# Empty slots' rows left out of an expert gather, and low parts moved from VectorE to GpSimd, in a two-block layer stack on one core

## The chip, the core and the metric

The kernel runs on one core of a Trainium2 chip. The time is that of one execution on the device, in microseconds; a kernel's time is the median of several runs. Of the core's engines, PE (TensorE) multiplies, DVE (VectorE), ACT (ScalarE) and POOL (GpSimd) work elementwise, and SP issues most loads. Each engine runs its own stream of instructions in order and waits on semaphores for the others. DMAs from the queues of SP, ACT and POOL run beside them.

## The reference, cut to what matters

Two blocks of a model work on 512 tokens of 1024 features in float32. The first block is attention of two kinds, cross-attention into a memory, and a mixture of experts; the second begins with a gated delta stage (with a short convolution and a memory attention of its own), followed by a feed-forward network, windowed attention and another network. The change touches the mixture of experts and the beginning of the delta stage.

```python
# experts: 4 groups of 8; each token takes one group and two experts in it
expert_ids = (g_sel * EXPERTS_PER_GROUP + e_sel).reshape(-1)      # 512 tokens x 2
def block_fn(args):
    tok, wt, e = args
    xb = h_pad[tok]                                   # the rows of one expert's tokens
    hidden = jax.nn.silu(xb @ w_gate[e]) * (xb @ w_up[e])
    return (hidden @ w_down[e]) * wt[:, None].astype(hf.dtype)
out = jnp.zeros((n_tok + 1, d), hf.dtype).at[slot_token].add(y.reshape(n_slots, d))[:n_tok]
x = x + out
x = rms_norm(x, norm_final_g)          # end of the first block
h = rms_norm(x, ln_mix_2)              # start of the second; its products with w_gdn and the small w_gdn_ba
```

(The last two lines are written in short; in the reference each norm stands in its own function.) An empty slot has no token, and its weight is zero.

## The kernel before, in words

Features lie on the partitions: the state x is eight tiles of 128 x 512 (feature chunk by token). Products are made nearly in float32 out of three products of rounded numbers: `split` (lines 404 to 411) takes a tile into a rounded high part (`hi`, on ACT) and the difference (`lo`, on DVE or on the engine that its argument names), and `mm3` (397 to 402) multiplies high by high, low by high and high by low. Weights come as tiles of 128 x 1024 (512 KB) through a ring of buffers; `use` makes their parts, `blk` runs one output tile of 128 x 512 over the eight chunks. A scheduler of the framework places each engine's instructions by dependences and by its own estimate of times; `issue_after(i)` holds what is written inside it back behind instruction i on the same engine.

**The mixture of experts** (`moe`, from line 1393). The router's product, then the choice of experts on DVE. Each expert has 64 slots, 2048 in all; two pairs of experts share a call of `slots`: on DVE four comparisons `G` (128 x 256, an iota against the tokens' positions), on PE eight small products `pm` that bring each slot its token number and weight, on DVE the token numbers `idx`, and on POOL two indirect DMAs that read the slots' token rows (128 rows of 4 KB each) from a copy of x in DRAM. An empty slot reads row 0. `gather` transposes these rows (`pgt`) on PE. Beside the choice of experts stand keys and values of a memory for the second block, for two layers (`mem_kv2`, 833 to 838): PE computes them, and they fill the time in which PE would have nothing. Then a branch (line 1697) tests for an expert with more than 64 tokens. The loop over experts follows: eight passes, each with four experts, `gate_up` (`pgu`), `down` (`py`), and `scatter` (`psx`), which adds the results to x through one-hot matrices `S`; DVE adds each `psx` into x (line 1651). Of the experts' weights, `NPRE` tiles are loaded ahead of the routing.

**The start of the delta stage** (`gdn`, from line 840). `two_norms` (from line 456) computes the statistics of two norms in one go: ACT squares the eight chunks (`sqt`), PE sums them (`sum`, line 471, two columns wide), DVE and POOL make the factors `rt`, and PE and DVE spread them to a row `rbc`. Meanwhile `xh` and `xl` are the parts of x for the products. `few` (from line 535) is the small product with `w_gdn_ba` (16 matmuls of 128 x 512, line 544), whose copy `fewo` is transposed (line 549). Then come the blocks with `w_gdn`; a block's result is multiplied with `rbc` into `pad` (944). The first blocks are not held. The second block of the stage has its first half behind the last sum product and its second half behind the product that makes `rbc` (`gates`, lines 525 to 528). Both results of `few` are put in the two banks (`pmm`) that the blocks use as well. The exponential `ea` of ACT (line 912) needs another function table than the squares.

## Time and profile before

| what | value |
|---|---|
| median of three runs | 2013.53 us (2011.08 to 2014.74) |
| the profiled execution | 2020.15 us |
| its span | 2018.4 us |
| mean granted clock of TensorE | 0.974 |
| PE busy (weight loads) | 96% (73%) |
| DVE, ACT, POOL busy | 51%, 37%, 18% |
| the chain that ended last | PE 69%, DVE 4%, ACT 2%, DMA 2% |
| DMA | 253.89 MB, mean 126 GB/s |

The profiled execution takes 1.75 us more than its span, which begins with the first instruction and ends with the last. The clock of TensorE has two levels, and the mean of 0.974 says that it was at the lower one for a twentieth of the time. A busy PE does not mean a PE at its best; a stretch must be looked at with its clock.

### The profile page before, as it was taken

How to read it: one execution, taken by the hardware profiler on the slowest of the kernel's cores; microseconds unless marked ns; L12 is line 12 of the kernel's file. 1: busy time of each engine (PE TensorE's matmuls, PEld its weight loads, DVE VectorE, ACT ScalarE, POOL GpSimd, SP SyncE). 2: the span in 40 equal slices, each digit the busy share in tenths (PEclk: the TensorE clock that was granted, in tenths of full speed). 3: DMA queues.
4: the chain of work that ended last, by engine and by line, in shares of the span. 5: the costliest groups of instructions: out<-in, count | busy, mean ns of one | idle time of the engine just before them, and what ended most of it. 6: DMA issues, size and time to landing. Idle time of an engine off the chain costs nothing.

```text
span 2018.4 us, 25671 instructions
## 1 busy us (share of the span) xinstructions
PE 1932.1 (96%) x9678; PEld 1471.1 (73%) x9678; DVE 1030.9 (51%) x2091; ACT 746.6 (37%) x1494; POOL 361.6 (18%) x344
## 2 busy tenths in 40 slices
PE   8999999979999999999998999999999999999997
PEld 6768677754444467878877888888866688888886
DVE  7674655643332367788856433343436654334434
ACT  5554643621212233345544322232335642222331
POOL 3012241200000003444412110111111021101111
PEclk9988999979999979999999999999999999999999
DMA  5213115259999832111122322332321033233322
GB/s 194 63 53 120 42 54 203 82 189 387 409 408 409 337 107 85 53 43 53 43 74 80 97 89 89 115 94 80 108 73 33 30 100 101 75 104 112 94 78 71
DMA packets 78911, 253.89 MB, mean 126 GB/s; under 512 B 9208, under 2 KB 12352, under 8 KB 78784
## 3 DMA queue, kind: packets, MB, share of 16 engines
q1 hardware_dynamic: 73520, 240.34, 34.7%
q0 software_dynamic: 2448, 8.43, 1.1%
q10 hardware_dynamic: 2816, 3.44, 0.5%
q8 instruction: 78, 1.28, 0.3%
q14 instruction: 49, 0.40, 0.1%
HBM read 243.75 MB, written 8.39 MB: 125 GB/s over the span
## 4 chain that ended last, share of the span: by engine, by line
PE 69%; DVE 4%; ACT 2%; DMA 2%; issue 1%; POOL 1%; DVEq 0%; ACTq 0%
PE mmp L400 16%; PE mmp L401 16%; PE mmp L402 16%; PE pgu L1599 6%; PE py L1599 3%; PE psx L1648 3%; DMA raw<-in_w_swa_dram 1%; PE sc L1327 1%; PE po L749 1%; DVE lo L408 1%; PE pgt L1446 1%; PE tp L961 1%; PE po L1353 1%; ACT hi L407 1%; PE pt L1339 1%
## 5 line engine op out<-in xcount | busy, mean ns | idle before, releaser
L400 PE MATMUL mmp<-xh,hi 128*128 128x512 f32 (+1 forms) x1328 | 522.1, 393 | 1.3 <-ACT xh L407 0.7
L401 PE MATMUL mmp<-xl,hi 128*128 128x512 f32 (+1 forms) x1328 | 516.0, 389 | 1.0 <-DVE xl L411 1.0
L402 PE MATMUL mmp<-xh,lo 128*128 128x512 f32 (+1 forms) x1328 | 516.1, 389 | 0.0
L407 ACT ACTIVATE hi<-raw 128x1024 fp32r<-128x1024 f32 (+2 forms) x256 | 252.1, 987 | 645.8 <-PE mmp L401 556.9
L408 DVE TENSOR_TENSOR lo<-raw,hi 128x1024 fp32r<-128x1024 f32 (+1 forms) x242 | 279.0, 1154 | 150.2 <-ACT hi L407 147.6
L400 PEld LDWEIGHTS mmp<-xh,hi 128*128 128x128 f32 x1328 | 252.0, 190 | 57.6 <-issue 5.7
L401 PEld LDWEIGHTS mmp<-xl,hi 128*128 128x128 f32 x1328 | 252.2, 190 | 50.1 <-DVE xl L411 1.4
L402 PEld LDWEIGHTS mmp<-xh,lo 128*128 128x128 f32 x1328 | 251.7, 190 | 50.2 <-issue 0.7
L808 POOL TENSOR_TENSOR g<-g,rbc 128x512 f32<-128x512 f32 x44 | 75.2, 1708 | 508.8 <-ACT g L807 508.8
L400 PE MATMUL mmp<-ahi,hi 128*128 128x512 f32 (+1 forms) x374 | 141.9, 380 | 0.0
L401 PE MATMUL mmp<-alo,hi 128*128 128x512 f32 (+1 forms) x374 | 141.9, 380 | 0.0
L402 PE MATMUL mmp<-ahi,lo 128*128 128x512 f32 (+1 forms) x374 | 141.9, 379 | 0.0
L434 POOL TENSOR_TENSOR sqt<-sqt 128x512 f32<-128x512 f32 (+1 forms) x50 | 70.0, 1399 | 255.9 <-ACT sqt L430 239.7
L810 DVE TENSOR_TENSOR a<-mmp,g 128x512 f32<-128x512 f32 x44 | 30.4, 691 | 144.4 <-PE mmp L402 144.4
L806 DVE TENSOR_TENSOR g<-mmp,rbc 128x512 f32<-128x512 f32 x44 | 30.4, 691 | 112.8 <-PE mmp L402 112.7
L401 PEld LDWEIGHTS mmp<-alo,hi 128*128 128x128 f32 x374 | 70.4, 188 | 14.1
L400 PEld LDWEIGHTS mmp<-ahi,hi 128*128 128x128 f32 x374 | 70.4, 188 | 14.0
L402 PEld LDWEIGHTS mmp<-ahi,lo 128*128 128x128 f32 x374 | 70.4, 188 | 14.0
L1599 PE MATMUL pgu<-raw,xh 128*64 128x512 f32 x256 | 61.0, 613 | 4.0 <-PEq L1697 4.0
L1599 PE MATMUL py<-raw,act 128*64 128x512 f32 x256 | 58.9, 596 | 1.0 <-ACT act L1626 1.0
L1599 PE MATMUL pgu<-raw,xl 128*64 128x512 f32 x256 | 57.2, 595 | 0.0
L410 ACT ACTIVATE xh<-py,msl 128x512 fp32r<-128x512 f32 x32 | 22.0, 688 | 94.8 <-PE py L1599 94.8
(519 smaller groups left out, 2969.6 us busy)
## 6 DMA issues: line engine op xcount, KB each, us to landing
raw<-in_w_egu_dram SPq DMA_DIRECT2D x128, 512.0 KB, 10.2
raw<-in_w_gu_dram SPq DMA_DIRECT2D x88, 512.0 KB, 3.5
raw<-in_w_ed_dram SPq DMA_DIRECT2D x64, 512.0 KB, 10.2
raw<-in_w_out_dram SPq DMA_DIRECT2D x24, 512.0 KB, 3.5
raw<-in_w_gdn_dram SPq DMA_DIRECT2D x24, 512.0 KB, 3.6
raw<-in_w_dn_dram SPq DMA_DIRECT2D x32, 384.0 KB, 3.1
raw<-in_w_dn_dram SPq DMA_DIRECT2D x32, 320.0 KB, 2.8
raw<-in_w_qk_dram SPq DMA_DIRECT2D x12, 512.0 KB, 4.3
```

The source lines that it names most:

```text
L400: mm(ps, a[0], b[0], start=first, stop=False)
L401: mm(ps, a[0], b[1], start=False, stop=False)
L402: mm(ps, a[1], b[0], start=False, stop=last)
L407: nc.scalar.activation(hi, src, AF.Copy)
L408: (eng or nc.vector).tensor_tensor(lo, src, hi.bitcast(F32), OP.subtract)
L410: nc.scalar.activation(hi, src, AF.Copy, scale=scale)
L434: (nc.vector if i == len(chunks) - 1 else nc.gpsimd).tensor_tensor(acc, acc, s, OP.add)
L806: nc.vector.tensor_tensor(g, pg, bc, OP.mult)
L808: nc.gpsimd.tensor_tensor(g, g, bc, OP.mult)
L810: nc.vector.tensor_tensor(a, pu, g, OP.mult)
L1599: m = nc.tensor.matmul(ps[hb], a[:, hb], w[b][:, o:o + 512], start=first, stop=last)
L1648: m = nc.tensor.matmul(psx, ys[k][:, a, c * P:(c + 1) * P], ss[a], start=a == part[0] and k == 0, stop=a == part[-1] and k == 1)
```

## The change

It has six parts.

1. In `slots` an empty slot gets the index 1023 instead of 0, and the indirect DMA checks its indices against 511 and skips a row beyond it. The row tiles are now fixed ones, set to zero once on POOL: two before the first gather, four behind the branch.
2. `mem_kv2` runs the first layer's keys and values early, and holds the second layer's keys behind the count product, its values behind the first `pm` products. The second layer's four low parts are made on POOL.
3. `NPRE` is 14 instead of 12.
4. In the delta stage the low parts of `w_gdn_ba` and of the first two tiles of `w_gdn` are made on POOL.
5. `few` is written inside `two_norms`' pool of banks and has a bank of its own there; the blocks' first half has no gate, the second half stands behind the last sum product.
6. `ea` is held behind the last Square.

```diff
-NPRE=12
+NPRE=14
...
-            self.split(hi, lo, t, eng=self.lo_eng)
+            self.split(hi, lo, t, eng=self.nc.gpsimd if self.lo_first else self.lo_eng)
+            self.lo_first = max(0, self.lo_first - 1)
...
-                if self.nblk == 2:
+                if self.nblk == 2 and self.loose:
+                    if c * 2 >= kc:
+                        st.enter_context(self.tc.issue_after(self.gates[0]))
+                elif self.nblk == 2:
...
-    def few(self, w, hs, pool):
+    def few(self, w, hs, pool, bank=None):
...
-        self.split(st[:, :, 0:64], st[:, :, 64:128], raw)
-        ps = self.pmm.tile([P, T], F32, name="mmp", tag="mm")
+        self.split(st[:, :, 0:64], st[:, :, 64:128], raw, eng=self.nc.gpsimd if self.lo_first else None)
+        bank = bank or (lambda name: self.pmm.tile([P, T], F32, name=name, tag="mm"))
+        ps = bank("mmp")
...
-    def mem_kv2(self, m):
+    def mem_kv2(self, m, l, gates):
...
-        for l in range(2):
-            self.mem_keys(m, d[f"w_mem_k2{l}"], 256, self.kv2d[l])
-            self.mem_values(m, d[f"w_mem_v2{l}"], 256, self.kv2d[l])
+        for g, f, w in zip(gates, (self.mem_keys, self.mem_values), (f"w_mem_k2{l}", f"w_mem_v2{l}")):
+            with self.tc.issue_after(g) if g else ExitStack():
+                f(m, d[w], 256, self.kv2d[l])
...
                 hs, rt, rbc, r1bc = self.two_norms("norm_final_g", "ln_mix_20", q, gp)
+                self.lo_first = 2
+                pba = self.few(d["w_gdn_ba"], hs, gp, lambda name: q.tile([P, T], F32, name=name, tag="few"))
...
-                nc.scalar.activation(ea, rows[:, 6:12], AF.Exp)
+                with tc.issue_after(self.squared):
+                    nc.scalar.activation(ea, rows[:, 6:12], AF.Exp)
...
+                far = gq.tile([P, 2], F32, name="far", tag="far", bufs=3)
+                nc.vector.tensor_scalar(far, ms[:, :, 4], 0.0, 1024.0, op0=OP.is_equal, op1=OP.mult)
                 idx = gq.tile([P, 2], I32, name="idx", tag="idx", bufs=3)
-                nc.vector.tensor_scalar(idx, ms[:, :, 4], 1.0, 0.0, op0=OP.subtract, op1=OP.max)
-                rows = []
+                self.idx = nc.vector.scalar_tensor_tensor(idx, ms[:, :, 4], -1.0, far, op0=OP.add, op1=OP.add).ins
                 for a in range(2):
-                    r = room() if room else gr.tile([P, D], F32, name="rows", tag="rows")
-                    nc.gpsimd.indirect_dma_start(r, None, tokd, bass.IndirectOffsetOnAxis(idx[:, a:a + 1], 0))
-                    rows.append(r)
+                    nc.gpsimd.indirect_dma_start(rows[a], None, tokd, bass.IndirectOffsetOnAxis(idx[:, a:a + 1], 0),
+                                                 bounds_check=T - 1, oob_is_err=False)
...
+                    self.mem_kv2(m2, 0, (None, None))
...
+                first = [r1.tile([P, D], F32, name=f"rows{a}") for a in range(2)]
+                for t in first:
+                    nc.gpsimd.memset(t, 0.0)
...
-                sl = slots(0, lambda: r1.tile([P, D], F32, name="rows", tag="rows", bufs=2), ps)
+                sl = slots(0, first, ps)
                 if self.on("gdn"):
-                    self.mem_kv2(m2)
+                    self.lo_eng = nc.gpsimd
+                    self.mem_kv2(m2, 1, (counts, self.pm))
+                    self.lo_eng = None
...
-            gr = e(name="mr", bufs=4)
+            gr = e(name="mr", bufs=1)
+            room = [gr.tile([P, D], F32, name=f"row{a}") for a in range(4)]
+            for t in room:
+                nc.gpsimd.memset(t, 0.0)
```

How this moves the instructions shows at three places. The first is POOL's stream in the routing, before the change: `sqt` and `rt` belong to norms, `rows` are the gathered rows, and `flag` is the branch's test.

```order
L434 TENSOR_TENSOR sqt<-sqt 128x256
L419 TENSOR_TENSOR rt<-rp,mhalf 128x4
L434 TENSOR_TENSOR sqt<-sqt 128x256 x5
L419 TENSOR_TENSOR rt<-rp,mhalf 128x2
L1430 DMA rows<-tokd,idx 128x1024 x2
L1696 TENSOR_LOAD flag
```

The same place after it:

```order
L437 TENSOR_TENSOR sqt<-sqt 128x256
L422 TENSOR_TENSOR rt<-rp,mhalf 128x4
L437 TENSOR_TENSOR sqt<-sqt 128x256 x5
L422 TENSOR_TENSOR rt<-rp,mhalf 128x2
L411 TENSOR_TENSOR lo<-raw,hi 128x1024 x4
L1438 DMA rows_3966<-tokd,idx 128x1024
L1438 DMA rows_3967<-tokd,idx 128x1024
L1713 TENSOR_LOAD flag
```

Four low parts now stand ahead of the two row DMAs. The second place is DVE's stream in the routing, before: `As` and `posm` are the tokens' positions in their experts, `mk` the copied keys, `msl` the slots' data.

```order
L408 TENSOR_TENSOR lo<-raw,hi 128x1024
L1559 TENSOR_TENSOR meta<-wt,meta 128x16x2 x4
L408 TENSOR_TENSOR lo<-raw,hi 128x1024
L1544 TENSOR_SCALAR As<-As 128x128
L1545 TENSOR_TENSOR posm<-pl,As 128x128
L1547 TENSOR_REDUCE mx<-posm 128x1
L1414 TENSOR_TENSOR G<-cst_moe,posm 128x256 x4
L694 TENSOR_TENSOR mk<-mmp,rbc 128x256
L1414 TENSOR_TENSOR G<-cst_moe,posm 128x256 x4
L408 TENSOR_TENSOR lo<-raw,hi 128x1024
L1550 TENSOR_REDUCE mx<-pl 1x1
L694 TENSOR_TENSOR mk<-mmp,rbc 128x256
```

After:

```order
L1571 TENSOR_TENSOR meta<-wt,meta 128x16x2 x4
L1556 TENSOR_SCALAR As<-As 128x128
L1557 TENSOR_TENSOR posm<-pl,As 128x128
L1559 TENSOR_REDUCE mx<-posm 128x1
L1422 TENSOR_TENSOR G<-cst_moe,posm 128x256 x8
L701 TENSOR_TENSOR mk<-mmp,rbc 128x256
L1562 TENSOR_REDUCE mx<-pl 1x1
L1563 CAST flag<-mx 1x1
L1431 COPY msl<-pm 128x16
```

The three low parts are gone from between, and all eight comparisons stand together. The third place is PE at the end of the sums, before, with the tiles' numbers: `sum0` to `sum3` are the four banks of sums, `mmp_6549` is the small product's bank, `mmp_6596` the first block's.

```order
L471 MATMUL sum3_6436<-gg_6409,sqt_6479 128x2
L544 MATMUL mmp_6549<-xl_6424,hi_6546 128x512
L544 MATMUL mmp_6549<-xh_6423,hi_6546 128x512
L544 MATMUL mmp_6549<-xl_6424,hi_6546 128x512
L544 MATMUL mmp_6549<-xh_6423,hi_6546 128x512
L544 MATMUL mmp_6549<-xl_6424,hi_6546 128x512
L544 MATMUL mmp_6549<-xh_6423,hi_6546 128x512
L544 MATMUL mmp_6549<-xl_6424,hi_6546 128x512
L549 MATMUL mmp_6568<-cst_all_113,fewo_6566 128x64 x4
L400 MATMUL mmp_6596<-xh_6413,hi_6592 128x512
L401 MATMUL mmp_6596<-xl_6414,hi_6592 128x512
```

After, with `mmp_6640` the first block's bank; of the small product nothing is left here but the transposes:

```order
L474 MATMUL sum3_6480<-gg_6453,sqt_6523 128x2
L404 MATMUL mmp_6640<-xl_6458,hi_6636 128x512
L405 MATMUL mmp_6640<-xh_6457,lo_6637 128x512
L403 MATMUL mmp_6640<-xh_6457,hi_6636 128x512
L404 MATMUL mmp_6640<-xl_6458,hi_6636 128x512
L405 MATMUL mmp_6640<-xh_6457,lo_6637 128x512
L403 MATMUL mmp_6640<-xh_6457,hi_6636 128x512
L556 MATMUL mmp_6584<-cst_all_113,fewo_6582 128x64 x4
L404 MATMUL mmp_6640<-xl_6458,hi_6636 128x512
L405 MATMUL mmp_6640<-xh_6457,lo_6637 128x512
L403 MATMUL mmp_6640<-xh_6467,hi_6636 128x512
L404 MATMUL mmp_6640<-xl_6468,hi_6636 128x512
```

Before, seven products of the small product stood behind the last sums, and the first block began behind its transposes. Now the small product stands between the earlier sums (with four products of the block), and the block's products stand on both sides of the transposes.

## Rows read from the trace of the kernel before

**Rows 1.** Windows: us; busy us (instructions) of PE, PEld, DVE, ACT, POOL; granted clock; DMA.

```profile
436.50:453.50 17.00, 9.02 (x28) 3.80 (x30) 0.97 (x2) 6.16 (x10) 0.00 (x0) 0.50 0.35 140
460.00:700.00 240.00, 232.00 (x1096) 105.19 (x1094) 75.52 (x156) 53.86 (x116) 12.29 (x13) 1.00 1.02 403
716.00:726.00 10.00, 8.94 (x47) 5.21 (x43) 6.79 (x19) 6.04 (x10) 0.14 (x2) 1.00 0.43 127
726.50:750.30 23.80, 22.79 (x81) 19.75 (x81) 11.08 (x38) 7.93 (x16) 2.05 (x2) 0.50 0.27 97
750.50:760.00 9.50, 9.50 (x51) 8.14 (x50) 7.12 (x18) 1.68 (x2) 0.00 (x0) 1.00 0.16 48
760.00:1090.00 330.00, 312.79 (x1730) 258.58 (x1729) 239.45 (x494) 147.74 (x336) 119.96 (x161) 0.99 0.19 61
```

**Rows 2.** Timeline of PE, routing to first pass: start, us, instruction, [idle before <- releaser].

```profile
438.06 0.66 PE L1446 MATMUL pgt<-cst_all,rows 128*128 128x128 f32 x2 [5.06 <-DMA rows<-tokd,idx]
440.48 0.69 PE L1446 MATMUL pgt<-cst_all,rows 128*128 128x128 f32 x2 [1.75 <-DMA rows<-tokd,idx]
...
449.18 6.61 PE L1599 MATMUL pgu<-raw,xh 128*64 128x512 f32 x20 [4.04 <-PEq L1697]
...
470.82 0.66 PE L1446 MATMUL pgt<-cst_all,rows 128*128 128x128 f32 x4
```

**Rows 3.** Waits of PE, 705 to 719 us: total, times, longest.

```profile
PE psx L1648 <- DVE x L1651: 2.1, 2, 1.3
```

**Rows 4.** Timeline of PE at the start of the delta stage.

```profile
727.11 5.28 PE L471 MATMUL sum<-gg,sqt 128*128 128x2 f32 x24 [0.32 <-ACT sqt L469]
...
745.24 1.97 PE L549 MATMUL mmp<-cst_all,fewo 128*128 128x64 f32 x8 [0.69 <-ACT fewo L546]
```

**Rows 5.** Timeline of DVE in the routing.

```profile
419.31 1.22 DVE L408 TENSOR_TENSOR lo<-raw,hi 128x1024 fp32r<-128x1024 f32 x1 [3.05 <-ACT hi L407]
...
426.05 1.22 DVE L408 TENSOR_TENSOR lo<-raw,hi 128x1024 fp32r<-128x1024 f32 x1
...
429.20 0.15 DVE L1426 TENSOR_SCALAR idx<-msl 128x2 int32<-128x2 f32 x1
```

**Rows 6.** Timeline of POOL in the routing.

```profile
430.23 1.23 POOL L1430 DMA_INDIRECT rows<-tokd,idx  x1 [19.94 <-DMA raw<-in_w_egu_dram]
431.76 0.95 POOL L1430 DMA_INDIRECT rows<-tokd,idx  x1 [0.30 <-PE mmp L402]
```

**Rows 7.** Instructions of the split's line on POOL: min/median/max ns.

```profile
L408 POOL TENSOR_TENSOR lo<-raw,hi x12: 1300/2394/2418, 186.9 to 299.7; 128x1024 fp32r<-128x1024 f32 x11, 128x512 fp32r<-128x512 f32 x1
```

**Rows 8.** The tile rows: landing of the gathered rows' DMAs.

```profile
DMA to landing us min/median/max: 3.5/8.5/10.7
```

**Rows 9.** Timeline of all engines in the first block, 283 to 285 us.

```profile
283.38 2.41 POOL L408 TENSOR_TENSOR lo<-raw,hi 128x1024 fp32r<-128x1024 f32 x1
...
284.70 1.64 DVE L411 SCALAR_TENSOR_TENSOR xl<-x,smt,xh 128x512 fp32r<-128x512 f32 x1
```

**Rows 10.** Timeline of DVE around the start of the delta stage.

```profile
709.10 1.22 DVE L408 TENSOR_TENSOR lo<-raw,hi 128x1024 fp32r<-128x1024 f32 x1
...
711.44 1.21 DVE L408 TENSOR_TENSOR lo<-raw,hi 128x1024 fp32r<-128x1024 f32 x1
...
723.19 0.74 DVE L411 SCALAR_TENSOR_TENSOR xl<-x,gg,xh 128x512 fp32r<-128x512 f32 x1
724.92 0.16 DVE L936 CAST head<-cst_gdn 18x6 fp32r<-18x6 f32 x1 [0.99 <-DMA cst_gdn<-in_cst_gdn_dram]
...
755.24 0.69 DVE L944 TENSOR_TENSOR pad<-mmp,rbc 128x512 f32<-128x512 f32 x1 [0.90 <-PE mmp L402]
```

**Rows 11.** Timeline of ACT around the start of the delta stage.

```profile
723.37 1.28 ACT L912 ACT_TABLE_LOAD   x1
725.11 0.21 ACT L912 ACTIVATE ea<-rows 128x6 f32<-128x6 f32 x1 [0.46 <-DMA rows<-in_rows_dram]
...
732.49 0.63 ACT L469 ACTIVATE sqt<-x 128x512 f32<-128x512 f32 x1 [0.46 <-PE sum L471]
```

More of the change, by code (lines that the diff above doesn't have):

```diff
@@ L289, in __init__ @@
         self.early = []
-        self.lo_eng = None
+        self.lo_first = 0
+        self.lo_eng, self.loose = None, False
     def on(self, ph):
@@ L468, in two_norms @@
             s = self.sq.tile([P, T], F32, name="sqt", tag="sq")
-            nc.scalar.activation(s, self.x[c], AF.Square)
+            self.squared = nc.scalar.activation(s, self.x[c], AF.Square).ins
             for t in range(4):
@@ L483, in two_norms @@
         rows = lambda: bank.tile([P, T], F32, name="stp", tag="mm")
-        self.gates, self.nblk = [m.ins], NB1
+        self.gates, self.nblk, self.loose = [m.ins], NB1, True
         self.rows_of(rbc, rt, rows())
@@ L505, in start @@
             r = (hs,) + self.xstats(q, both)
-        self.nblk = 0
+        self.nblk, self.loose = 0, False
         return r
@@ L546, in few @@
         nc.scalar.activation(o, ps, AF.Copy)
-        pt = self.pmm.tile([P, T], F32, name="mmp", tag="mm")
+        pt = bank("mmp")
         for t in range(4):
@@ L849, in gdn @@
                 hs, rt, rbc, r1bc = self.two_norms("norm_final_g", "ln_mix_20", q, gp)
+                self.lo_first = 2
+                pba = self.few(d["w_gdn_ba"], hs, gp, lambda name: q.tile([P, T], F32, name=name, tag="few"))
+                ba = gp.tile([P, 4, 12], F32, name="ba")
+                nc.vector.tensor_tensor(ba, pba[:, :, 0:12], rt.unsqueeze(2).to_broadcast([P, 4, 12]), OP.mult)
             for c in range(8):
@@ L866, in gdn @@
             nc.scalar.dma_start(rows, d["rows2"][:, 0:12].to_broadcast([P, 12]))
-            pba = self.few(d["w_gdn_ba"], hs, gp)
             G = lambda name: gp.tile([P, 4, 6], F32, name=name)
-            ba = gp.tile([P, 4, 12], F32, name="ba")
             beta, hbeta, gc, eg, kgs, egl = (G(name) for name in ("beta", "hbeta", "gc", "eg", "kgs", "egl"))
@@ L876, in gdn @@
             f2 = lambda t: t.rearrange("p a b -> p (a b)")
-            nc.vector.tensor_tensor(ba, pba[:, :, 0:12], rt.unsqueeze(2).to_broadcast([P, 4, 12]), OP.mult)
             mark = {}
@@ L1408, in moe, with slots @@
             gq = e(name="mg", bufs=2)
-            def slots(q, room=None, bank=None):
+            def slots(q, rows, bank=None):
                 G = gq.tile([P, 4, 256], F32R, name="G", tag="G")
@@ L1419, in slots @@
                     for t in range(4):
-                        nc.tensor.matmul(pm[:, 8 * a:8 * a + 8], G[:, t, P * a:P * a + P], meta[:, t, 2 * q + a],
-                                         start=t == 0, stop=t == 3)
+                        self.pm = nc.tensor.matmul(pm[:, 8 * a:8 * a + 8], G[:, t, P * a:P * a + P], meta[:, t, 2 * q + a],
+                                                   start=t == 0, stop=t == 3).ins
                 ms = gq.tile([P, 2, 8], F32, name="msl", tag="msl", bufs=3)
                 nc.vector.tensor_copy(ms, pm[:, 0:16].rearrange("p (a b) -> p a b", a=2))
+                far = gq.tile([P, 2], F32, name="far", tag="far", bufs=3)
+                nc.vector.tensor_scalar(far, ms[:, :, 4], 0.0, 1024.0, op0=OP.is_equal, op1=OP.mult)
                 idx = gq.tile([P, 2], I32, name="idx", tag="idx", bufs=3)
-                nc.vector.tensor_scalar(idx, ms[:, :, 4], 1.0, 0.0, op0=OP.subtract, op1=OP.max)
-                rows = []
+                self.idx = nc.vector.scalar_tensor_tensor(idx, ms[:, :, 4], -1.0, far, op0=OP.add, op1=OP.add).ins
                 for a in range(2):
-                    r = room() if room else gr.tile([P, D], F32, name="rows", tag="rows")
-                    nc.gpsimd.indirect_dma_start(r, None, tokd, bass.IndirectOffsetOnAxis(idx[:, a:a + 1], 0))
-                    rows.append(r)
+                    nc.gpsimd.indirect_dma_start(rows[a], None, tokd, bass.IndirectOffsetOnAxis(idx[:, a:a + 1], 0),
+                                                 bounds_check=T - 1, oob_is_err=False)
                 nc.vector.tensor_tensor(ms[:, :, 0:2], ms[:, :, 0:2], ms[:, :, 2:4], OP.add)
@@ L1540, in moe @@
                 for k in range(1, 4):
-                    nc.tensor.matmul(pc[:, 32 * k:128], self.ones, Af[:, 0:128 - 32 * k], start=False, stop=k == 3)
+                    counts = nc.tensor.matmul(pc[:, 32 * k:128], self.ones, Af[:, 0:128 - 32 * k], start=False, stop=k == 3).ins
                 pf = posm.rearrange("p a b -> p (a b)")
@@ L1661, in moe @@
             self.pe = None
-            sl = slots(1)
+            sl = slots(1, room[0:2])
             sg = gate_up(0, *g)
@@ L1678, in moe @@
                         if q < 6:
-                            sl = slots(q + 2)
+                            sl = slots(q + 2, room[2 - q % 2 * 2:4 - q % 2 * 2])
                 act = turned(nx)
```

## The prediction

> **What bounds the kernel now.** The profiled run took 2020.15 us, 1.75 us of it outside the span. I read the table of windows first, around the two places that the diff touches. PE is the engine to watch: it is busy 232.0 of 240 us in the expert loop (460 to 700), at full clock, and 312.8 of 330 us in the delta stage (760 to 1090). In two short stretches between these it is idle, or slow: from 436.5 to 453.5 it is busy 9.02 of 17 us, from 726.5 to 750.3 it is busy 22.79 of 23.8, and in both the granted clock is 0.50, the lower of its two levels (1.2 GHz, not 2.4); in the windows around the second it is 1.00 [rows 1].
>
> PE's timeline says what ends the idle time of the first place: 5.06 and 1.75 us on the DMAs of the gathered rows, then 4.04 us on the branch of the overflow test [rows 2]. At the second place the waits say 2.1 us for DVE's additions into x [rows 3], and the timeline 0.69 us for the copy of the small product [rows 4].
>
> **Place A, routing to the first expert (395 to 455 us).** Removed from DVE: the low parts of the second layer's memory keys and values. Two of the four stand at 419.31 and 426.05, 1.22 us each [rows 5], and one between them. On POOL the same shape takes 2.39 us [rows 7]. Moved: the count product, ahead of those keys, some 0.9 us earlier. Added: one tiny DVE operation, two memsets on POOL long before, four behind the branch.
>
> For DVE alone that is a gain. Counts at 419.5, then rescaling, positions, their maximum and four G of 0.36 us: the first pair's G would be done near 422.6. The index then stands behind the copy of the keys, whose products end near 427.3, so idx comes near 428.0 (before 429.20 [rows 5]) and the first row DMA leaves near 429 (before 430.23 [rows 6]).
>
> A row speaks against it. While POOL computes a low part (283.38, 2.41 us), a DVE operation with two inputs in SBUF that starts at 284.70 takes 1.64 us [rows 9]; the same form alone takes 0.74 [rows 10]. It ends 0.55 us after POOL's, so it stood until POOL was nearly through. A G compares two SBUF tiles, so it is such an operation. With ACT's present times three of the four moved low parts become ready just where As and the G stand. As would end near 421.9, behind the first of the three; the first G at 424.4, behind the second; one more may slip in before the third, which holds POOL to 427.2; the fourth G ends near 427.9. PE meets the pm products in the middle of the keys, so it stands about 2.5 us there, the keys end near 429.7, and idx comes near 432.6, after the copies and the next pair's four G. The Trainium skill, SBUF — State Buffer, section Who interferes with whom, states this as an exclusive hold on shared ports, for the whole instruction, between a GpSimd instruction that reads SBUF and a DVE instruction with two SBUF inputs. The 1.64 us row agrees; by that rule idx is the late one, without it the early one, 4.6 us apart. I take the late one, since [rows 9] shows the wait.
>
> Rows' transfers: 1024 of the 2048 slots hold a token, so about half of each 512 KB goes. Before, the second transposes start at 440.48, 8.7 us after the issue at 431.76 [rows 2, 6]; the sixteen landings run from 3.5 to 10.7 us, median 8.5 [rows 8]. I take 6 us, nearer to the middle: half the bytes go, and two more weight loads are over by then. The Trainium skill, DMA: Bandwidth & Descriptors, section Anatomy of one DMA, gives 2.0 us plus bytes over 436 GB/s; by that, half of 512 KB would save an estimated 0.6 us only. No row here shows a half transfer.
>
> Second DMA issued near 435, landed near 441, against 440.48: +0.5. The next pair's eight pm products stand before the branch now, no longer in the first pass: about 1 us here, 1 us less there, 0. Branch and low clock stay: 0. A costs +0.5. Bounds: early idx and a landing of 3.5 us put the row at 434, -6.5; late idx and 10.7 us, +5.5.
>
> **The expert loop.** Half the rows take 0.5 MB a pass out of transfers of 403 GB/s, but PE is 97% busy there [rows 1]: 0. The four memsets stand ahead of the second pair's DMAs on POOL. Those rows are first read at 470.82, 21 us after PE has passed the branch [rows 2]. If a memset took as long as a low part, 2.39 us [rows 7], the four would be over in 10 us, and a landing of 8.5 would still be in time: 0.
>
> **Place B, end of the loop to the delta stage (700 to 756 us).** DVE loses three low parts that stand between the additions into x, two of them 1.22 and 1.21 us long [rows 10]. POOL is idle there, and the additions read PSUM, so they are not of the kind of [rows 9]. PE's waits go: -2.1 us at this point [rows 3]. ACT's table load, 1.28 us, and the exponential with its wait, 0.46 and 0.21, move behind the last Square [rows 11]; the Squares end 2.1 + 1.95, some 4 us earlier, near 729 instead of 733.1. DVE's wait for constants (0.99 us [rows 10]) stays where it is, so the last scatter product starts near 723.8, 2.2 us earlier.
>
> From there to the end of the first block PE has 64 records of sums, 16 of the small product, 8 of transposes and 24 of the block. At the low clock 24 sums take 5.28 us and the transposes 1.97 [rows 4]; at twice that speed, with 0.23 us for a product of 512 columns, it is 7.0 + 3.7 + 1.0 + 5.5, about 17 us. Each microsecond at the low clock adds half of one. With the 23.8 us of before the block would end at 723.8 + 17 + 12 = 752.8; before, it ended just under 755.24 [rows 10]. The order is better too: the small product and ten of the block's products now lie between the sums, where PE ran two-column products alone, and the block waits neither for the small product's copy (0.69) nor for its banks. I take a low stretch of 19 us, ending near 750: -5.5. Bounds: full clock throughout, 741, -14; low all the way, 758, +2.5. The first pad waits some 1.6 us more for the copied norm row; the second block's 5.5 us of products hide that, since its first half no longer waits for the sums. Without that cover it would cost the 1.6.
>
> **The delta stage.** The same instructions, partly in another order. PE idles 17 of 330 us there [rows 1]; I count 0, with 3 us either way.
>
> **Sum.** +0.5 - 5.5 = -5.0: the profiled run would take 2015.15. The median shown lies 6.6 us below the profiled run; from it, 2013.53 - 5.0 = **2008.5**.
>
> **Rivals.**
> (1) The clock stays up at place B, or returns at once, because wide products are spread more evenly. For it: 716 to 726 has 8.94 us of work and a clock of 1.00 [rows 1]. Against it: the wide scatter products end earlier now, and the sums stay. -14 at B, +0.5 at A: 2000.
> (2) POOL doesn't hold up DVE, and the rows come soon: A gives -5, B -5.5: 2003. Against it speak [rows 9].
> (3) The gain is hidden: PE's work at B slides into an equally long low stretch (23.8 us, -2.4), and A's rows come 1.5 us later than I take (+2): no change, 2013. For it: the clock came back before only after an unbroken run of wide products, and sums still break it.
> (4) Slower: POOL's low parts hold DVE at A, PE stands on the pm products, and the row DMAs leave near 434 and 435 from behind them on POOL's queue. If skipped rows save no time (landing 8.5 us [rows 8]), A costs +3, and at 10.7 it costs +5.5; with the low clock to the block's end (+2.5) the kernel takes 2019 to 2021.5, and 2017 if B gives nothing. It decides once A costs more than B gives.
>
> **Numbers.** A difference of 0.2%, 4 us, is about what a measurement of this kernel can tell from no change. Forecast (-1.5 to -9 us): 0.44, of which 0.32 lie beyond -4 us. (1) 0.12 and (2) 0.06, both faster; (3) 0.20, no change; (4) 0.18, slower. Faster 0.50, same 0.32, slower 0.18. The range runs from 1998, a little below (1), to 2018, into (4); the forecast's own is 2004.5 to 2012.
>
> **What would show it.** At A: G of 1 to 2.5 us beside POOL's low parts, PE idle before pm, idx after 431; an idx before 429 would prove the blocking wrong. First rows landing near 6 us; at 8 or more, the bytes did not matter. At B: no wait of PE on the x additions after 705, the last Square ended near 729, the first pad near 751.5, the low stretch shorter than 23.8 us. The forecast is wrong if that stretch is as long as before, if the delta stage moves by more than 3 us, or if PE begins to wait for expert weights.

## The result, and the profile after

| | before | after |
|---|---|---|
| median of the runs | 2013.01 us (4 runs) | 2025.27 us (4 runs) |
| lowest and highest | 2011.08, 2014.74 | 2023.40, 2031.97 |
| the profiled execution, its span | 2020.15, 2018.4 us | 2031.97, 2030.2 us |

The changed kernel is slower: the ratio is 1.0052 with an interval of 1.0032 to 1.0072. The forecast was 2008.5 us with a range to 2018; the direction was wrong as well. The change does what its words say. From the page of after, its first part and the DMA queues (q0 is POOL's queue with the gathered rows): the rows' bytes fell to 4.24 MB, where the page of before has 8.43 for this queue, and POOL is at 19% where it was at 18%.

```profile
PE 1938.3 (95%) x9678; PEld 1476.9 (73%) x9678; DVE 1034.0 (51%) x2092; ACT 746.1 (37%) x1493; POOL 390.2 (19%) x357
...
q0 software_dynamic: 2448, 4.24, 0.6%
```

To see where time went I set the two traces side by side by PE's work: the columns of all matmuls were added up from the start, and at each instant of before I read when the other trace had done the same sum. The difference is how late the other is. What each stretch adds to it, in us (stretches in the times of before; these are worked out from the traces' matmul records, not printed by a view; inside the delta stage, where the orders differ, a border between two stretches can move its figures by some 0.5 us):

```
start to 335     +1.3        700 to 760  (place B)            -2.2
335 to 395       -2.8        760 to 1095 (delta stage)        +8.9
395 to 460  (A)  +4.2           of it 760-785 +2.7, 785-975 -3.4, 975-1000 +5.4, 1000-1095 +4.2
460 to 700       -0.8        1095 to the end                  +3.3
```

These add up to the 11.9 us between the two profiled executions (11.82). The largest term is the stage that the prediction counted at nothing.

**Place A.** The hold by POOL is there. DVE's timeline of after, routing (columns as in [rows 5]), which answers to [rows 5]: the first eight G take 6.50 us. Two of them stand until just after a low part of POOL ends, 1.99 and 2.58 us; one slips in between, and the last five start when POOL is through. Three of the next four, with POOL idle, take 1.07, 0.36 each. `idx` starts at 432.04.

```profile
409.09 2.09 DVE L1508 TENSOR_TENSOR e1o<-ep,e1v 128x32 f32<-128x32 f32 x1
...
413.10 0.19 DVE L1508 TENSOR_TENSOR e2o<-ep,e2v 128x32 f32<-128x32 f32 x1
...
421.02 1.35 DVE L1556 TENSOR_SCALAR As<-As 128x128 f32<-128x128 f32 x1 [4.55 <-PE pl L1553]
...
422.93 6.50 DVE L1422 TENSOR_TENSOR G<-cst_moe,posm 128x256 fp32r<-128x256 f32 x8
...
430.15 1.07 DVE L1422 TENSOR_TENSOR G<-cst_moe,posm 128x256 fp32r<-128x256 f32 x3
...
432.04 0.14 DVE L1436 SCALAR_TENSOR_TENSOR idx<-msl,far 128x2 int32<-128x2 f32 x1
```

The same timeline in narrower windows (422.9 to 424.8, and 425.3 to 427.6) shows the two G that stand:

```profile
422.93 1.99 DVE L1422 TENSOR_TENSOR G<-cst_moe,posm 128x256 fp32r<-128x256 f32 x1
...
425.18 2.58 DVE L1422 TENSOR_TENSOR G<-cst_moe,posm 128x256 fp32r<-128x256 f32 x1
```

POOL's timeline of the same stretch, which answers to [rows 6]: low parts at 408.79 and from 419.90 to 427.5 stand beside the slow DVE instructions, and the row DMAs leave at 432.49 and 434.07, some 2.3 us later than before.

```profile
408.79 2.35 POOL L411 TENSOR_TENSOR lo<-raw,hi 128x1024 fp32r<-128x1024 f32 x1
419.90 4.74 POOL L411 TENSOR_TENSOR lo<-raw,hi 128x1024 fp32r<-128x1024 f32 x2 [8.76 <-ACT hi L410]
425.03 2.45 POOL L411 TENSOR_TENSOR lo<-raw,hi 128x1024 fp32r<-128x1024 f32 x1 [0.39 <-ACT hi L410]
432.49 1.29 POOL L1438 DMA_INDIRECT rows<-tokd,idx  x1 [5.01 <-DVE msl L1443]
434.07 0.99 POOL L1438 DMA_INDIRECT rows<-tokd,idx  x1 [0.30 <-ACT mv L2226]
452.25 4.19 POOL L1597 MEMSET row<- 128x1024 f32 x4 [17.18 <-PEq L1714]
```

PE's waits from 395 to 455 us (total, times, longest): the third and the last line are the hold's price on PE, 4.5 us, of which before had 1.1 (the wait for `mk`); the rows' wait stayed (6.8 before [rows 2]), and the branch's fell from 4.0 to 2.9.

```profile
PE pgt L1454 <- DMA rows<-tokd,idx: 6.6, 2, 4.1
PE pgu L1616 <- PEq L1714: 2.9, 1, 2.9
PE mmp L403 <- DVE mk L701: 2.5, 1, 2.5
PE pm L1428 <- DVE G L1422: 2.0, 2, 1.2
```

The gathered rows, landing times of the tile, which answer to [rows 8], and below it PE's timeline at the two transposes, which answers to [rows 2]. The first gather's rows are transposed from 6.1 us after its issue on (438.55 - 432.49), the second's from 9.0 (443.08 - 434.07), no sooner than before (8.7).

```profile
DMA to landing us min/median/max: 5.2/5.9/9.0
```

```profile
438.55 0.41 PE L1454 MATMUL pgt<-cst_all,rows 128*128 128x128 f32 x2 [2.50 <-DMA rows<-tokd,idx]
443.08 0.69 PE L1454 MATMUL pgt<-cst_all,rows 128*128 128x128 f32 x2 [4.11 <-DMA rows<-tokd,idx]
```

**Place B.** PE's waits on x from 705 to 719 us fell from 2.1 us [rows 3] to 0.2; but in the next stretch, 719 to 728, one of 2.0 us stands on the addition queued behind DVE's wait for constants (0.4 there before). First 705 to 719, then 719 to 728:

```profile
PE psx L1665 <- DVE x L1668: 0.2, 1, 0.2
```

```profile
PE psx L1665 <- DVE x L1668: 2.0, 1, 2.0
```

The windows of after (columns as in [rows 1]) show place B, the whole delta stage and three places in it:

```profile
726.50:750.30 23.80, 23.18 (x98) 20.57 (x96) 8.46 (x22) 8.98 (x14) 2.05 (x2) 0.59 0.28 98
760.00:1090.00 330.00, 310.42 (x1712) 257.15 (x1711) 239.53 (x492) 141.85 (x327) 119.64 (x155) 0.98 0.19 58
770.00:790.00 20.00, 18.05 (x94) 14.91 (x94) 13.81 (x26) 6.79 (x13) 11.66 (x13) 1.00 0.25 71
975.00:1010.00 35.00, 32.36 (x207) 26.45 (x206) 31.00 (x73) 18.12 (x54) 19.07 (x24) 1.00 0.14 45
1040.00:1075.00 35.00, 31.44 (x138) 25.03 (x137) 19.57 (x32) 11.62 (x21) 1.74 (x4) 0.95 0.25 75
```

The last three windows of before. PE is hardly idle there, and the clock never falls:

```profile
770.00:790.00 20.00, 20.00 (x101) 16.50 (x99) 16.22 (x22) 7.67 (x12) 12.06 (x13) 1.00 0.27 81
975.00:1010.00 35.00, 34.98 (x217) 28.60 (x216) 27.61 (x70) 17.93 (x53) 12.23 (x20) 1.00 0.15 46
1040.00:1075.00 35.00, 34.18 (x150) 27.70 (x149) 19.14 (x26) 9.74 (x14) 1.54 (x2) 1.00 0.30 91
```

**The first place in the delta stage** is the gates' two small products, `gc` and then `gr`, with DVE work between them. PE's timeline before: ten wide products (of 512 columns) stand between `gc` (768.10) and the second `gc` (770.71), and nobody waits.

```profile
768.10 0.38 PE L915 MATMUL gc<-gg,cst_gdn 128*128 128x24 f32 x2
768.33 0.48 PE L402 MATMUL mmp<-xh,lo 128*128 128x512 f32 x1
...
770.71 0.30 PE L917 MATMUL gc<-gc,cst_gdn 128*128 128x24 f32 x2
770.85 0.28 PE L931 MATMUL gr<-cst_all,part 128*72 128x128 f32 x1
```

After, the scheduler has set them side by side, and PE stands 1.25 and 0.70 us while DVE makes what lies between. (In e1 to e4 below, which have this too, the granted clock falls as well: it is 0.89 from 765 to 780, and 1.00 in after's execution.)

```profile
770.55 0.38 PE L923 MATMUL gc<-gg,cst_gdn 128*128 128x24 f32 x2
772.18 0.40 PE L925 MATMUL gc<-gc,cst_gdn 128*128 128x24 f32 x2 [1.25 <-DVE gc L924]
773.28 0.27 PE L939 MATMUL gr<-cst_all,part 128*72 128x128 f32 x1 [0.70 <-DVE part L937]
```

**The second place** is the last heads of the stage. After, PE's timeline: the products of 512 columns that lay between one head's small products are used up early. Around 990 no such product is left between the small ones, and PE stands for DVE's `cv` and ACT's `on`:

```profile
989.61 0.66 PE L969 MATMUL tp<-cst_all,cv 128*128 128x128 f32 x4 [0.74 <-DVE cv L963]
...
995.11 0.33 PE L1179 MATMUL pb<-cst_all,on 128*128 128x128 f32 x1 [0.92 <-ACT on L1177]
```

Around 1050 it stands 1.88 us for `on` and 0.79 for `mixt`; then seven products of 512 columns in a row take 0.63 us instead of 0.39, at the lower clock.

```profile
1047.45 0.49 PE L1168 MATMUL pb<-S,qgT 128*128 128x128 f32 x2 [0.61 <-DVE fm L1180]
...
1050.04 0.33 PE L1179 MATMUL pb<-cst_all,on 128*128 128x128 f32 x1 [1.88 <-ACT on L1177]
1051.16 0.82 PE L403 MATMUL mmp<-mixt,hi 128*128 128x512 f32 x2 [0.79 <-ACT mixt L410]
1051.78 0.63 PE L404 MATMUL mmp<-mixt,hi 128*128 128x512 f32 x1
```

Before, a `pb` near 990 and the last one come with wide products ahead of them and wait for nothing; only `mixt` is waited for:

```profile
992.57 0.27 PE L1171 MATMUL pb<-cst_all,on 128*128 128x128 f32 x1
...
1042.95 0.27 PE L1171 MATMUL pb<-cst_all,on 128*128 128x128 f32 x1
1044.04 0.73 PE L400 MATMUL mmp<-mixt,hi 128*128 128x512 f32 x2 [0.82 <-ACT mixt L407]
```

For the work that before does from 975 to 1060, after needs some 10 us more (973.6 to 1068.6). PE is idle for 8.0 us there, where before has 3.2; the 3.4 us at the lower clock cost 1.7 by an estimate from its half speed; the rest, some 3.5 us, is busy time, which I put down to small products that follow each other with no wide ones among them; no run shows that apart.

The instructions after the delta stage stand in the same order in both kernels. Of the 3.3 us after 1095, most goes with two stretches of 3.4 us at the lower clock that before's execution doesn't have (at 1495 and 1577); since nothing moved there, and e1 below, with the same order from 760 on, has neither (-0.4 us), while e5 and e8 have one each (at 1472 and 1482), I take them for chance.

### The profile page after: what moved, and what is told of

Same layout as the page of the kernel before. It is cut to its first block, busy times and chain, and to the rows that moved or that the text cites. A ratio compares the mean times of both kernels' runs of the same rounds, so it can differ in the third digit from the quotient of the medians.

```text
span 2030.2 us, 25705 instructions
## 1 busy us (share of the span) xinstructions
PE 1938.3 (95%) x9678; PEld 1476.9 (73%) x9678; DVE 1034.0 (51%) x2092; ACT 746.1 (37%) x1493; POOL 390.2 (19%) x357
## 3 DMA queue, kind: packets, MB, share of 16 engines
q0 software_dynamic: 2448, 4.24, 0.6%
## 4 chain that ended last, share of the span: by engine, by line
PE 68%; DVE 4%; ACT 2%; DMA 2%; POOL 1%; issue 1%; DVEq 0%; ACTq 0%; POOLq 0%
PE mmp L403 15%; PE mmp L404 15%; PE mmp L405 15%; PE pgu L1616 6%; PE py L1616 3%; PE psx L1665 3%; DMA raw<-in_w_swa_dram 1%; PE sc L1335 1%; DVE lo L411 1%; PE po L756 1%; PE tp L969 1%; PE pgt L1454 1%; PE po L1361 1%; DVE cv L957 1%; ACT hi L410 1%
## 5 line engine op out<-in xcount | busy, mean ns | idle before, releaser
L411 DVE TENSOR_TENSOR lo<-raw,hi 128x1024 fp32r<-128x1024 f32 (+1 forms) x236 | 273.3, 1159 | 146.9 <-ACT hi L410 146.5
## 6 DMA issues: line engine op xcount, KB each, us to landing
raw<-in_w_egu_dram SPq DMA_DIRECT2D x128, 512.0 KB, 10.2
```

Of the source, the lines that this page charges most:

```text
L411: (eng or nc.vector).tensor_tensor(lo, src, hi.bitcast(F32), OP.subtract)
```

## The experiments

Before and after stand in one scheduler's order, so a part of the change can act far from where it is written. The theory after the result: the small product written earlier (part 5) changes the scheduler's order through the whole delta stage, and that order costs the time. Rivals: POOL's hold at the routing (part 2), and a loss in the row transfers (part 1). e1 to e4 share their runs of before, and so do e5 to e8 and e9 to e12. Before's medians in these three groups are 2014.95, 2016.38 and 2015.26 us; the ratio of a row belongs to its group's runs of before and is not the quotient of the two medians. Beside it, the table has four stretches of each profiled execution, worked out as above, in us against before's.

```
                       median   ratio [95% interval]       A     B   760-785  975-1095
after                 2025.27  1.0052 [1.0032, 1.0072]   +4.2  -2.2   +2.7     +9.6
e1_bank_only          2027.99  1.0049 [1.0030, 1.0068]   -1.7  -1.8   +4.9     +9.6
e2_delta_only         2020.55  1.0023 [1.0010, 1.0036]   -1.6  -2.1   +3.8     +0.1
e3_without_keys       2017.38  1.0005 [0.9992, 1.0018]   -0.1  -0.7   +3.7      0.0
e4_keys_on_dve        2024.52  1.0038 [1.0026, 1.0051]   +2.7  -5.8   +4.7     +9.7
e5_no_bank            2011.16  0.9974 [0.9963, 0.9986]   -1.5  -9.1    0.0     +0.3
e6_prefetch_rows      2016.47  0.9998 [0.9988, 1.0009]    0.0  -2.9    0.0     +0.3
e7_keys_on_pool       2018.63  1.0015 [1.0005, 1.0025]   +0.9  -2.8    0.0      0.0
e8_keys_order         2016.84  0.9999 [0.9988, 1.0011]   +0.8  -4.5    0.0      0.0
e9_table6             2014.18  0.9999 [0.9986, 1.0011]   +4.7  -2.3   +1.4     +0.2
e10_table7            2022.98  1.0047 [1.0029, 1.0064]   -1.6  -2.2   +0.7     +9.6
e11_table6_dve        2015.07  0.9997 [0.9986, 1.0009]   +1.9  -7.7   +1.4     +1.0
e12_no_keys_no_bank   2012.53  0.9989 [0.9977, 1.0000]   +0.1  -5.7   +0.1     +1.0
```

**e1_bank_only**: before, with the small product early and in its own bank, nothing else.

```diff
                 hs, rt, rbc, r1bc = self.two_norms("norm_final_g", "ln_mix_20", q, gp)
+                pba = self.few(d["w_gdn_ba"], hs, gp, lambda name: q.tile([P, T], F32, name=name, tag="few"))
...
-            pba = self.few(d["w_gdn_ba"], hs, gp)
```

> The kernel before with one part of the change: the small product is written inside the norms' pool and has its own bank. Nothing of the routing is touched; PE's order in the delta stage is instruction for instruction that of the changed kernel, which differs from that of before at about 1160 places. Theory 1 (the order that the scheduler gives the delta stage costs the time): the delta stage is 8 to 10 us longer from 760 to 1090, as in the changed kernel (8.9), the start of the stage gains about 2, so about 7 us over before, 2020. Theory 2 (the loss in the delta stage comes from what the engines do there: POOL's low parts, the ungated half): none of that is here, so within 2 us of before, 2011 to 2015.

Measured 1.0049, more than the 7 us expected. This one edit alone loses as much as the whole change. PE's order in the delta stage is that of after, and both places are there.

**e2_delta_only**: after, without parts 1 to 3; the parts at the start of the delta stage (4 to 6) stay.

```diff
-NPRE=14
+NPRE=12
...
-                    self.mem_kv2(m2, 1, (counts, self.pm))
+                    self.mem_kv2(m2, 1, (None, None))
...
-                    nc.gpsimd.indirect_dma_start(rows[a], None, tokd, bass.IndirectOffsetOnAxis(idx[:, a:a + 1], 0),
-                                                 bounds_check=T - 1, oob_is_err=False)
+                    nc.gpsimd.indirect_dma_start(r, None, tokd, bass.IndirectOffsetOnAxis(idx[:, a:a + 1], 0))
```

> The kernel before with all parts of the change at the start of the delta stage (low parts on POOL, own bank, no gate for the first half, the exponential behind the last Square), nothing of the routing. The scheduler gives the delta stage nearly the order of before here (about 150 places differ, against 1160). Theory 1 (order): the start gains 2 to 5 us, the rest costs nothing, 2008 to 2011. Theory 2 (the parts themselves cost time in the delta stage): 6 to 9 us slower, 2019 to 2022.

Measured 1.0023: the median lies in theory 2's range and not in theory 1's, which had counted the gates' products at nothing. They stand side by side (+3.8), yet the order of the last heads is that of before (about 150 places differ in the stage, against some 1160 in after), and the 9.6 us are gone. Whether the 3.8 us come from the order or from the parts, this run can't tell; e9 can.

**e3_without_keys**: after, without part 2.

```diff
-                    self.mem_kv2(m2, 0, (None, None))
...
-                    self.lo_eng = nc.gpsimd
-                    self.mem_kv2(m2, 1, (counts, self.pm))
-                    self.lo_eng = None
+                    self.mem_kv2(m2, 0, (None, None))
+                    self.mem_kv2(m2, 1, (None, None))
```

> The changed kernel without its second part: keys and values of the memory stand where they stood before, low parts on DVE. The delta stage's order comes out near that of before again (about 150 places differ). Theory 1 with the lock on the ports at the routing: no blocked comparisons (first row DMA at 429 to 430), rows some 2 us earlier, the 2.7 us of the cross-attention kept, the start of the delta stage better by 2: 2006 to 2009. Theory 2 (delta stage's parts cost): about 8 us more than that, 2015 to 2017.

Measured 1.0005, again near theory 2's figure. Taken alone this looks like proof that the keys on POOL cost the time; but the order of the last heads went back as well, and the rows of the table show that this gives back 9.6 us and place A 4.3, in executions where A moves by 6 us without any edit (below).

**e4_keys_on_dve**: after, with the second layer's low parts on DVE.

```diff
-                    self.lo_eng = nc.gpsimd
+                    self.lo_eng = None
```

> The changed kernel with the second layer's four low parts of the memory on DVE instead of POOL; all else as in the changed kernel, with its order of the delta stage. Theory 3 (POOL's low parts hold up DVE's comparisons in the routing, which costs 4 of the 12 us): first row DMA back near 429 to 430, PE's waits on comparisons and copied keys (2.0 and 2.5 us) gone, 3 to 4 us faster than the changed kernel, 2021 to 2022. Rival (the routing loses for another reason: the branch, the low clock, the row transfers): within 1 us of the changed kernel, 2024 to 2026. By theory 1 it stays slower than before in either case, by 8 us or more.

Measured 1.0038, where the rival put it: the 3 to 4 us of theory 3 did not come. The hold is gone and the first row DMA leaves at 428.13 instead of 432.49, but the second one's rows are transposed only 10.5 us after its issue. Most of the loss stays, with after's order in the stage.

**e5_no_bank**: after, with the small product back behind the norms and in the common banks.

```diff
-                pba = self.few(d["w_gdn_ba"], hs, gp, lambda name: q.tile([P, T], F32, name=name, tag="few"))
...
+            pba = self.few(d["w_gdn_ba"], hs, gp)
```

> The changed kernel with one part undone: the small product stands again where it stood before and shares the blocks' two banks. The routing is as in the changed kernel; PE's order in the delta stage comes out as before (10 places differ, against 1160). Theory 1 (the delta stage loses by the order that follows from the early small product: waits and low clock at the gates' products near 770 to 780, and twice 4.5 us near 990 and 1050): 9 to 12 us faster than the changed kernel, within 3 us of before. Rival (the delta stage loses by POOL's low parts or by the ungated half): still 8 us or more over before.

Measured 0.9974, the whole interval below 1: this version is faster than both kernels, more than expected. In PE's delta stage 10 places differ from before, and neither loss is there.

**e6_prefetch_rows**: before, with parts 1 and 3.

```diff
-NPRE=12
+NPRE=14
...
-                    nc.gpsimd.indirect_dma_start(r, None, tokd, bass.IndirectOffsetOnAxis(idx[:, a:a + 1], 0))
+                    nc.gpsimd.indirect_dma_start(rows[a], None, tokd, bass.IndirectOffsetOnAxis(idx[:, a:a + 1], 0),
+                                                 bounds_check=T - 1, oob_is_err=False)
```

> The kernel before with two parts of the change: 14 weight tiles ahead instead of 12, and empty slots' rows left out (fixed row tiles, memsets). The delta stage has exactly the order of before. Theory (the cross-attention gains 2 to 3 us from its order with the longer prefetch, and the rows land some 2 us sooner at the routing): 3 to 5 us faster than before. Rival (both are hidden: the cross-attention's gain is a matter of where the low clock falls, and PE waits for the branch in any case): within 1.5 us of before.

Measured 0.9998. The landing's median falls to 5.4 us, and the time doesn't move: neither a gain nor the rival's loss.

**e7_keys_on_pool** and **e8_keys_order**: before, with part 2; in e8 the low parts stay on DVE (`None` for `nc.gpsimd`).

```diff
+                    self.mem_kv2(m2, 0, (None, None))
...
-                    self.mem_kv2(m2)
+                    self.lo_eng = nc.gpsimd
+                    self.mem_kv2(m2, 1, (counts, self.pm))
+                    self.lo_eng = None
```

> The kernel before with the second part of the change alone: the order of the memory's keys and values, and the second layer's low parts on POOL. The delta stage has exactly the order of before. Theory 3 (POOL's low parts hold up DVE's comparisons at the routing): the first row DMA leaves 2 to 4 us later than at 430.2, PE waits on comparisons and copied keys, 3 to 5 us slower than before. Rival (no hold-up; three low parts of 1.22 us off DVE): idx near 428, 1 to 2 us faster.

> The same as the kernel with the keys on POOL, but with the low parts on DVE: only the order of the keys and values is changed. Theory 3: no comparison is held up, the first row DMA leaves at 429 to 430, within 1.5 us of before, and 3 to 5 us faster than with the low parts on POOL. Rival (it is the order that costs, not POOL): as slow as with the low parts on POOL.

Measured 1.0015 and 0.9999. In e7's profile PE's waits in the routing are after's (2.5 and 2.0 us):

```profile
PE mmp L403 <- DVE mk L701: 2.5, 1, 2.5
PE pgt L1453 <- DMA rows<-tokd,idx: 2.5, 2, 1.3
PE pm L1427 <- DVE G L1421: 2.0, 2, 1.2
```

In e8 the wait for `G` is not among the listed ones and that for `mk` is 1.1. The hold is real in PE's waits. The ratios differ by 0.0016, 3.2 us (the medians by 1.8), with intervals that overlap, so its price in the whole is not shown.

**e9_table6** and **e10_table7**: after, with one number of the kernel's table of holds (line 25) changed, to 6 in e9 and to 7 in e10. `z0:g2:4` holds one output block's chunks from the fifth on behind the product `gr`, so that they don't run before it. With the small product early, the number decides how many wide products are left for the place between the gates' products.

```diff
-GG="z0:g2:4"
+GG="z0:g2:6"
```

> The changed kernel, all parts, with one number of the delta stage's table set from 4 to 6: the block z0 stands behind the product gr from its seventh chunk on, not from its fifth. The scheduler now puts six products between the two gc products (one before the change of the number: none) and gives the rest of the delta stage nearly the order of before (109 places differ). Theory 1 (the time is lost by order alone, at two places: the gates' products side by side, about 4 us, and the later heads' order, about 9): 10 to 13 us faster than the changed kernel, 2010 to 2015. Rival (the own bank, the ungated half or POOL's low parts cost by themselves): 2020 or more.

> As the kernel with the number 6, but with 7: nine products lie between the two gc products, yet the rest of the delta stage keeps the changed kernel's order (153 places differ from it, 1219 from before). It tells the two places of theory 1 apart: the 4 us at the gates' products come back, the 9 us of the later heads stay, so about 4 us faster than the changed kernel, 2020 to 2023. Rival (the gates' products are the whole loss, and the later heads follow from it): 2010 to 2015, as with 6.

Measured 0.9999 and 1.0047, both as expected. Nothing that after computes or moves is taken out in e9, all its parts are in, and the loss is gone: that rules out the parts themselves as its cause. Windows of e9 at the three places; the last two are as full as before's:

```profile
770.00:790.00 20.00, 19.04 (x101) 15.92 (x100) 15.80 (x28) 7.32 (x13) 11.39 (x13) 1.00 0.27 81
975.00:1010.00 35.00, 34.96 (x219) 28.87 (x218) 28.21 (x69) 18.03 (x54) 13.73 (x21) 1.00 0.15 46
1040.00:1075.00 35.00, 33.72 (x151) 27.16 (x149) 20.61 (x29) 10.69 (x16) 1.54 (x2) 1.00 0.29 87
```

e10 tells the two places apart. Between the gates' products lie nine wide ones, where e9 has six (+0.7 us), but the last heads stand as in after, and the kernel is nearly as slow as after. So the last heads' order carries the loss, and the gates' products the smaller part.

**e11_table6_dve**: e9 with the second layer's low parts on DVE (the edit of e4).

> The kernel with the number 6 and the second layer's low parts of the memory on DVE. The two causes found, the order and POOL's hold on the comparisons, are both out. Theory: 2 to 3 us faster than the kernel with the number 6, 2008 to 2012, faster than before. Rival (the hold at the routing is hidden by the rows' transfers): the same as with the number 6.

Measured 0.9997 against e9's 0.9999, as the rival said: no price of POOL's hold shows here. With e7 against e8 (0.0016) and after against e4 (0.0014), the three pairs put it at 0.4 to 3.2 us.

**e12_no_keys_no_bank**: after, without part 2 and with the small product back (the edits of e3 and e5).

> The changed kernel without its second part (the memory's keys as before) and without the own bank. The delta stage's order is nearly that of before (26 places). Theory: as the kernel without the bank (2011) less the 2 to 3 us of POOL's hold on the comparisons: 2008 to 2010. Rival (the hold is hidden): 2011 to 2013.

Measured 0.9989, as the rival said, against e5's 0.9974 with the keys on POOL. The intervals overlap: no cost of part 2 shows here, nor a gain.

## Why the prediction was wrong

**The step that failed** is the paragraph on the delta stage: "The same instructions, partly in another order. [...] I count 0, with 3 us either way." The order was the change there. Measured: +8.9 us in the profiled execution, made of +2.7 at the gates' products, +9.6 at the last heads and -3.4 between. The last heads cost 9.6 to 9.7 us in each of the four kernels with after's order (after, e1, e4, e10) and 0 to 1.0 in the nine others, and the medians follow: 1.0038 to 1.0052 against 0.9974 to 1.0023. The prediction took PE's 17 us of idle time in 330 [rows 1] for a sign that order matters little; it showed that the order of before was a good one, and so had something to lose. That the two small products stood side by side was to be read from PE's new order; that this would cost a wait followed from DVE's work between them.

**Place A, +4.2 instead of +0.5.** The mechanism was right: G of 1.99 and 2.58 us beside POOL's low parts, PE standing before `pm`, `idx` after 431 (432.04; predicted 432.6). The rule of the Trainium skill, SBUF — State Buffer, section Who interferes with whom, an exclusive hold between the two engines, is borne out: 1.99 and 2.58 against 0.36 us for a G, each ending 0.28 us after POOL's instruction. But PE ran 1.4 us ahead of before at 395, so in before's times `idx` came at 433.5. And the term of the landing failed: I took 6 us for both gathers. The first took 6.1; the second, which ends the wait, 9.0. These 0.9 and 3.0 us are the 3.7 that the term was off, within the reading. Over all thirteen changed kernels, from the issue to the transposes, the second landing took 8.4 to 8.9 us in the four with full rows (e1, e2, e7, e8) and 4.6 to 10.5 in the nine with half rows: half the bytes, but on the mean 8.1 us against 8.6. e10 runs after's instructions in A, in the same order, and there the second gather's rows are transposed 4.8 us after its issue (438.25 - 433.48), with a wait of 0.36:

```profile
437.28 0.62 PE L1454 MATMUL pgt<-cst_all,rows 128*128 128x128 f32 x2 [0.32 <-DMA rows<-tokd,idx]
438.25 0.44 PE L1454 MATMUL pgt<-cst_all,rows 128*128 128x128 f32 x2 [0.36 <-DMA rows<-tokd,idx]
```

A then gives -1.6 instead of +4.2; e5 and e9, with the same order there, have -1.5 and +4.7, with 4.6 and 9.3 us for the second gather. So A's term is 6 us wide between executions of the same instructions. Of it, 4.2 us (9.0 - 4.8) are this transfer; 1.3 are its issue, which comes earlier in e10, where the granted clock from 395 to 430 is 0.89 and not 0.80. Why the transfer lands so differently stays open.

**The expert loop, 0.** Right: 232.0 busy us of 240 before and after, no wait of PE for weights among the listed ones. The four memsets took 4.19 us, under the bound of 10.

**Place B, -2.2 instead of -5.5.** The waits on x from 705 to 719 went, and the last scatter product came where it was forecast: at 726.06, with after 1.9 us behind before at 700, 724.1 in before's times (predicted 723.8). The rest did not follow. The last Square ended at 740.06, not near 729, because it waited for sums that now stand behind products of 512 columns; the first `pad` started at 757.21, not 751.5. Four of the block's products lie between the sums, not ten; six stand behind them. The sum was off too: 723.8 + 17 + 9.5 is 750.3, which is 4.9 us under 755.24, not 5.5. The clock was low from 727 to 751 with one break of 3.4 us, 20.5 us in all where I took 19: near enough, and yet worth little.

More instructive is what I compared with. The stretch of 23.8 us at the lower clock [rows 1] was taken as a property of the kernel. e6, e7 and e8 leave the start of the delta stage as it was, and they have 13.7 to 17.1 us of low clock there, and B 2.8 to 4.5 us shorter; the windows of e7 and of e8:

```profile
726.50:750.30 23.80, 22.23 (x94) 19.16 (x94) 11.60 (x37) 9.25 (x18) 2.05 (x2) 0.64 0.29 105
```

```profile
726.50:750.30 23.80, 22.28 (x101) 18.53 (x102) 14.12 (x49) 8.60 (x17) 2.05 (x2) 0.71 0.30 112
```

The profiled execution of before was 6.6 us above its median, and I subtracted from the median a gain worked out on it; part of that gain was in the median already.

**The rivals.** (4), slower by POOL's hold and a late landing at A, named a real mechanism, and after's profiled execution shows it; that it had the direction right is luck, for it is not the cause of the slower median: without the hold (e4) the loss stays, and with it (e9, e5) the kernel is as fast as before or faster. (1), the clock that returns at B, happened in e5 (10.2 us low, B -9.1) but not in after. No rival named the order of the delta stage; the prediction had a move of that stage by more than 3 us only as a sign of being wrong.

**Still open:** the price of POOL's hold (0 to 3 us by the three pairs, none clear of noise), what makes the second gather land late, and which of the parts left in e5 bring its 5 us; alone, parts 1 and 3 (e6) and part 2 (e7, e8) bring nothing.

## What to carry to other kernels

Where a scheduler orders the instructions, an edit's cost is also the new order of everything behind it: compare the new order with the old over the whole stage, and look for small products that now stand side by side with another engine's work between them, and for waits that have lost the wide products that filled them. Holds tuned by hand (here one number) belong to the order they were tuned on; tune them again before a part is judged, since e3 alone would have blamed the wrong part. Before a gain is worked out on one stretch of one profile, see how far that stretch moves between executions: a low clock or a late transfer may be this execution's, not the kernel's.

## What the runs showed of the hardware that was not expected

- POOL's hold reached instructions that the prediction had not priced: a TENSOR_TENSOR of 128 x 32 took 2.09 us beside a low part and 0.19 alone, a TENSOR_SCALAR of 128 x 128 took 1.35 us beside one and 0.22 alone (before, at 422.25).
- A memset of 128 x 1024 on POOL takes about 1.05 us (four in 4.19), less than half of a low part of that shape (2.4).
- Skipping half of a gather's rows halved its bytes (8.43 to 4.24 MB on the queue) and left the rows of the second of two gathers ready (their transposes started) 4.6 to 10.5 us after its issue, against 8.4 to 8.9 with all rows.
- With the same instructions in the same order at place B, the time at the lower clock was 23.9 us in before's execution and 13.7 to 17.1 in those of e6, e7 and e8.
